# Sums of squares of queries and keys: one fp32 product with ones, or two fp32r products of a two-part split

## The chip, the cores and the metric

The kernel runs on one core of a Trainium2 chip. The metric is the device time of one execution in microseconds (us), taken as the median of several runs. Before the change it is 2640.64 us, the median of 3 runs (2636.08 to 2641.43).

Six names are used for what works side by side on the core: PE (TensorE, matrix products), PEld (TensorE's weight loads), DVE (VectorE), ACT (ScalarE), POOL (GpSimd) and SP (SyncE, which here issues the DMA transfers). Each of them works through its own list of instructions in order, and an instruction that must wait holds up all that stand behind it on the same engine.

## The reference

The reference is a two-layer backbone over 512 latent tokens and 256 context tokens. In each layer one combined input projection feeds three mixers: a neighbourhood attention, a gated DeltaNet with 4 heads of 128 channels, and a Fourier mixer; they are merged, projected, and followed by an MLP. The change lies in the DeltaNet's input, where queries and keys go through a short convolution with SiLU, are normalised to length one per head, and the latent ones are rotated:

```python
def _l2norm(x):
    xf = x.astype(jnp.float32)
    return xf * lax.rsqrt(jnp.sum(xf * xf, axis=-1, keepdims=True) + EPS)

q_l, k_l, v_l = _split(_short_conv(jnp.concatenate([dn_q, dn_k, dn_v], axis=-1), conv_w), (DN_W,) * 3)
lat_qkv = (_bhtd(_axial_rope(_l2norm(_heads(q_l, DN_HEAD_DIM)))),
           _bhtd(_axial_rope(_l2norm(_heads(k_l, DN_HEAD_DIM)))),
           _bhtd(_heads(v_l, DN_HEAD_DIM).astype(jnp.float32)))
...
k_c = _l2norm(_heads(k_c, DN_HEAD_DIM))
```

The context keys (and, in the first layer, the context queries) are normalised in the same way, without the rotation.

## The kernel before, in words

Activations lie with channels on the 128 partitions and tokens along the free dimension: 512 latent tokens and 256 context tokens, 768 in all. Large products are done in three fp32r products each (`proj`, L250 to L257): weights and inputs are split into a rounded part `hi` (ACT, L243) and a remainder `lo` (POOL or DVE, L246), both of type fp32r, and hi·hi, hi·lo and lo·hi are summed in PSUM.

A layer runs in stages. In the first stage (after L1042) the input projections of the first DeltaNet head stand beside the Fourier mixer. Then comes the mixed stage (L1059): four streams of work are written out side by side by `by_clock` (L340), which picks the stream that is least far along by the amounts that each `yield` gives: the recurrent steps of the DeltaNet (`stream_dn`), the preparation of a head with its triangular inverse (`stream_prep`, `dn_prep`), the neighbourhood attention (`stream_na`), and the input projections that feed them (`stream_in`). After it come merging, output projection and MLP, in which almost only `proj` runs. The compiler's scheduler then puts the instructions of each engine into their final order, by the priorities in which the program wrote them and by its own idea of when their inputs are ready. So a change of one instruction can move others.

`dn_in` (L523) makes one head's inputs. For the key it projects, runs `conv_silu` (L467: copy out of PSUM into `cin`, five taps on DVE, SiLU by exponentials on ACT, a last product on DVE at L482), then `l2_rope` (L485). That function squares the result on ACT (L488, into `r_l2`, 770 columns with a gap of two, or 512 where there are only latent tokens), sums the squares over the 128 channels with one fp32 product with a matrix of ones (L493: 512 columns, then 256), takes the sum to the power −1/2 by Ln and Exp on ACT (L494, L495), scales on DVE (L498, L500), and rotates (L502 to L507; the product with the sine is on POOL, L505, and that with the cosine on DVE, L506). The value goes through the convolution alone; the query goes through both again. There are 16 calls of `l2_rope`: a key and a query for each of four heads in two layers. Twelve have 770 columns; the four queries of the second layer have 512. The four calls of the two first heads lie in the first stages, twelve in the mixed ones.

The buffers with the tag `cy` (L962) hold `cin`, the result of the convolution, and `r_l2`, three in number.

Of the kernel before, what the change touches and what calls it, by code (L numbers as in the profile page):

```python
# [9 lines left out]
F32 = mybir.dt.float32  # L10
F32R = mybir.dt.float32r
AF = mybir.ActivationFunctionType
ALU = mybir.AluOpType
# [4 lines left out]
P = 128  # L18
# [28 lines left out]
def kernel(ctx: ExitStack, tc: tile.TileContext, A: dict, out: bass.AP):  # L47
    nc = tc.nc
    pe, dve, act, pool, sp = nc.tensor, nc.vector, nc.scalar, nc.gpsimd, nc.sync
# [3 lines left out]
    const = ctx.enter_context(tc.tile_pool(name="const", bufs=1))  # L53
# [12 lines left out]
    def U(name, dt=F32, tag="u", w=TT):  # L66
        b, n = cur[tag]
        return b.tile([P, w], dt, tag=tag, bufs=n, name=name)

    def T3(name):  # L70
        return U(name, tag="t3b")

    @contextmanager
    def scope(name, **bufs):
        with tc.tile_pool(name=name, bufs=1, reuse_waits="tile") as b:
            for t, n in bufs.items():
                cur[t] = (b, n)
            yield b
# [38 lines left out]
    xload(5)  # L117
    ones = const.tile([P, P], F32, name="ones")
    dve.memset(ones, 1.0)
    Tst = const.tile([P, NU, P], F32, name="Tst")  # L120
    pool.memset(Tst, 0.0)
    def sigmoid_into(dst, src):
# [252 lines left out]
    def layer(l):  # L375
# [109 lines left out]
        def l2_rope(y, w, scale, name, par):  # L485
            n = 770 if w > TL else 512
            r = U("r_l2", tag="cy", w=774)
            act.activation(out=r[:, :n], in_=y[:, :n], func=AF.Square)  # L488
            for s0, s1, o0 in ((0, TL, 0), (TL, TT, 514)):
                if s0 < w:  # L490
                    o1 = o0 + s1 - s0
                    ps = ps_aux("ps_l2")
                    pe.matmul(ps[:, 0:s1 - s0], lhsT=ones, rhs=r[:, o0:o1], start=True, stop=True)  # L493
                    act.activation(out=r[:, o0:o1], in_=ps[:, 0:s1 - s0], func=AF.Ln, bias=EPS)  # L494
                    act.activation(out=r[:, o0:o1], in_=r[:, o0:o1], func=AF.Exp, scale=-0.5)  # L495
            o = U(name, tag=name + par)
            kn = tp.tile([P, TL], F32, tag="t2", name="kn")
            dve.scalar_tensor_tensor(kn, in0=y[:, 0:TL], scalar=scale, in1=r[:, 0:TL], op0=ALU.mult, op1=ALU.mult)  # L498
            if w > TL:
                dve.scalar_tensor_tensor(o[:, TL:TT], in0=y[:, 514:770], scalar=scale, in1=r[:, 514:770],  # L500
                                         op0=ALU.mult, op1=ALU.mult)
            rot = tp.tile([P, TL], F32, tag="t2", name="rot")  # L502
            for q in range(4):
                sp.dma_start(out=rot[32 * q:32 * q + 32], in_=kn[32 * (q ^ 1):32 * (q ^ 1) + 32])
            pool.tensor_tensor(rot, rot, sinT, op=ALU.mult)  # L505
            dve.tensor_tensor(kn, kn, cosT, op=ALU.mult)  # L506
            dve.tensor_tensor(o[:, 0:TL], kn, rot, op=ALU.add)  # L507
            return o
# [450 lines left out]
                    yield 2  # L959


        mix_a = scope("mixa", **{f"{n}{i}": 1 for n in ("kT", "qT", "ktok", "vtok") for i in range(2)}, O=1, zz=1, cy=3)  # L962
        mix_a.__enter__()

        sts = [{} for _ in range(NDH)]
# [140 lines left out]
        for bi, (src, gt) in enumerate(((ofn, 16), (ona, 0), (odn, 8))):  # L1106
# [14 lines left out]
            for k in range(KD):  # L1121
# [3 lines left out]
                else:  # L1125
                    ps = inproj(T_GATE + gt + k, segs)
                    sigmoid_into(sg[:, :W], ps[:, :W])
                ada_tick(ADA_BR)
                ps = ps_main("ps_br")
                if bi == 0:  # L1130
                    proj_fn(ps, k)
                    y = ys[k] = U("y")
# [20 lines left out]
        for k in range(KD):  # L1153
# [3 lines left out]
            ps = ps_main("ps_wo")  # L1157
# [15 lines left out]
        for hb in range(4):  # L1173
            ah, al = [], []
            for k in range(8):
                ada_tick(ADA_M)
                ps = ps_main("ps_m1")
                proj(ps, wload(A["w1"][l, hb * 8 + k]), KD, mh, ml, segs)
                r = T3("rl")
# [3 lines left out]
                x, y = split_act(a[:, :W], W, "a", U)  # L1183
                ah.append(x)
                al.append(y)
            for k in range(KD):
# [3 lines left out]
                w = wload(A["w2"][l, hb, k])  # L1190
                end = hb == 3 and fin is not None

                for sg in [[s] for s in HALVES] if end and k == KD - 1 else [segs]:
                    ps = ps_main("ps_m2")
# [172 lines left out]
```

## Time and profile before

| what | value |
|---|---|
| median of 3 runs | 2640.64 us |
| profiled execution, its own time | 2641.14 us |
| span of the profiled execution | 2639.4 us |
| PE busy | 2460.9 us (93%) |
| DVE busy | 1516.9 us (57%) |
| ACT busy | 1194.3 us (45%) |
| POOL busy | 652.1 us (25%) |
| mean granted clock of TensorE | 0.974 |
| DMA, mean over the span | 106 GB/s |

The profile is of one execution. Busy time is what an engine spent in instructions, and the share is of the span. The end of a matmul is modelled, so that the duration shown for one is longer than the step from one to the next; where both are to be had, the step is what TensorE can give. "Idle before" is the time in which the engine waited just before the instructions of a group, and the name after the arrow is what ended most of that wait. The chain of waits follows the work that ended last back from the last instruction, at each step to what released it.

### The profile page before, as it was taken

What the parts mean: (1) busy time and instruction counts of PE and PEld (TensorE: products, weight loads), DVE (VectorE), ACT (ScalarE), POOL (GpSimd) and SP (SyncE); (2) the same over time, 40 slices, a digit from 0 to 9 for tenths busy, and PEclk for the clock granted to TensorE, in tenths of its full rate; (3) what the DMA queues carried; (4) which work ended last, traced back from release to release, by engine and by line L of the source; (5) the groups of instructions that cost most, each with busy time, mean ns of one, the idle gap of its engine ahead of it and who ended that gap; (6) DMA issues with size and microseconds to landing.
All of it is one profiled execution on the core that took longest, in us unless ns stands there. A gap on an engine that the chain in (4) does not pass through costs nothing.

```text
span 2639.4 us, 39034 instructions
## 1 busy us (share of the span) xinstructions
PE 2460.9 (93%) x14608; PEld 2043.2 (77%) x14608; DVE 1516.9 (57%) x2867; ACT 1194.3 (45%) x2445; POOL 652.1 (25%) x552
## 2 busy tenths in 40 slices
PE   6988989989998999999999988898889999999998
PEld 3776877777887878888888867776767777788886
DVE  5628575757457976564444473858668357433334
ACT  4545656565654233131313255555565653423333
POOL 3223222231122122111111133222242232222222
PEclk9999999999998999999999999999999999999999
DMA  7223232323155733333343313232232345233332
GB/s 223 71 80 87 69 83 61 90 79 82 63 186 166 222 121 120 118 119 120 120 128 119 117 56 97 78 86 69 82 89 74 111 134 190 78 96 96 96 96 88
DMA packets 190853, 280.89 MB, mean 106 GB/s; under 512 B 57876, under 2 KB 82200, under 8 KB 190536
## 3 DMA queue, kind: packets, MB, share of 16 engines
q1 hardware_dynamic: 190664, 278.40, 34.8%
q8 instruction: 114, 1.87, 0.3%
q14 instruction: 75, 0.61, 0.1%
HBM read 242.86 MB, written 26.03 MB: 102 GB/s over the span
## 4 chain that ended last, share of the span: by engine, by line
PE 69%; DVE 15%; ACT 5%; issue 4%; DMA 3%; POOL 2%; SPq 1%; DVEq 0%; POOLq 0%; ACTq 0%
PE ps_m L255 33%; PE ps_in L255 13%; PE ps_wo L255 4%; PE ps_inc L255 4%; PE ps_br L255 3%; DVE stmp L591 2%; DVE Wb L593 2%; DVE cy L479 2%; PE ps_s L827 1%; DVE Pm L809 1%; PE ps_ch L686 1%; PE ps_ch L682 1%; DVE xn L313 1%; PE ps_ch L704 1%; PE ps_s L821 1%
## 5 line engine op out<-in xcount | busy, mean ns | idle before, releaser
L246 POOL TENSOR_TENSOR wlo<-wr,whi 128x512 fp32r<-128x512 f32 x352 | 487.0, 1385 | 1679.8 <-ACT whi L243 1555.0
L243 ACT CAST whi<-wr 128x512 fp32r<-128x512 f32 x544 | 336.0, 619 | 778.0 <-PE ps_m L255 492.2
L255 PE MATMUL ps_in<-hh,whi 128*128 128x512 f32 x960 | 381.6, 408 | 27.1 <-ACT whi L243 21.6
L255 PE MATMUL ps_in<-hh,wlo 128*128 128x512 f32 x960 | 376.0, 402 | 2.8 <-POOL wlo L246 2.6
L255 PE MATMUL ps_in<-hl,whi 128*128 128x512 f32 x960 | 376.3, 403 | 0.0
L255 PE MATMUL ps_m<-ml,whi 128*128 128x512 f32 (+1 forms) x768 | 233.5, 358 | 4.5 <-POOL ml L323 3.9
L255 PE MATMUL ps_m<-mh,whi 128*128 128x512 f32 (+1 forms) x768 | 232.9, 358 | 4.4 <-ACT mh L319 4.4
L255 PE MATMUL ps_m<-ah,whi 128*128 128x512 f32 (+1 forms) x776 | 233.6, 354 | 0.0
L255 PE MATMUL ps_m<-ah,wlo 128*128 128x512 f32 (+1 forms) x776 | 233.2, 354 | 0.0
L255 PE MATMUL ps_m<-al,whi 128*128 128x512 f32 (+1 forms) x776 | 233.0, 354 | 0.0
L255 PE MATMUL ps_m<-mh,wlo 128*128 128x512 f32 (+1 forms) x768 | 232.1, 356 | 0.0
L255 PEld LDWEIGHTS ps_in<-hh,whi 128*128 128x128 f32 x960 | 182.2, 194 | 59.2 <-ACT whi L243 23.2
L246 DVE TENSOR_TENSOR wlo<-wr,whi 128x512 fp32r<-128x512 f32 x192 | 134.8, 702 | 139.9 <-ACT whi L243 139.9
L255 PEld LDWEIGHTS ps_in<-hh,wlo 128*128 128x128 f32 x960 | 180.4, 193 | 38.6 <-POOL wlo L246 5.4
L255 PEld LDWEIGHTS ps_in<-hl,whi 128*128 128x128 f32 x960 | 181.2, 193 | 29.9 <-issue 2.2
L1197 DVE SCALAR_TENSOR_TENSOR x<-ps_m,mod,x 128x512 f32<-128x512 f32 (+1 forms) x97 | 60.8, 654 | 215.4 <-PE ps_m L255 215.4
L202 DVE SCALAR_TENSOR_TENSOR jada<-wada,csb 128x1024 f32<-128x1024 f32 x128 | 179.6, 1403 | 0.9 <-DMA wada<-in_wat_dram 0.4
L255 PEld LDWEIGHTS ps_m<-ml,whi 128*128 128x128 f32 x768 | 127.8, 189 | 29.7 <-POOL ml L323 6.8
L255 PEld LDWEIGHTS ps_m<-mh,whi 128*128 128x128 f32 x768 | 127.7, 190 | 27.3 <-ACT mh L319 6.2
L255 PE MATMUL ps_inc<-hh,whi 128*128 128x256 f32 x512 | 148.8, 291 | 0.0
L255 PE MATMUL ps_inc<-hl,whi 128*128 128x256 f32 x512 | 148.8, 291 | 0.0
L255 PE MATMUL ps_inc<-hh,wlo 128*128 128x256 f32 x512 | 148.7, 290 | 0.0
(337 smaller groups left out, 4918.3 us busy)
## 6 DMA issues: line engine op xcount, KB each, us to landing
wr<-in_w_dram SPq DMA_DIRECT2D x256, 256.0 KB, 2.6
wr<-in_wi_dram SPq DMA_DIRECT2D x224, 256.0 KB, 2.8
wada<-in_wat_dram SPq DMA_DIRECT2D x80, 512.0 KB, 4.0
wr<-in_wb_dram SPq DMA_DIRECT2D x48, 256.0 KB, 3.0
wada<-in_wa_dram SPq DMA_DIRECT2D x32, 256.0 KB, 5.4
wr<-in_wo_dram SPq DMA_DIRECT2D x32, 256.0 KB, 2.9
gpre<-sgp SPq DMA_DIRECT2D x16, 384.0 KB, 2.3
sgg<-gpre SPq DMA_DIRECT2D x16, 384.0 KB, 4.0
```

The costliest lines, as they stand in the source:

```text
L202: pin(dve.scalar_tensor_tensor(junk, in0=ws[n], scalar=1.0, in1=cur["csb"][:, v * D:v * D + D], op0=ALU.mult, op1=ALU.mult, accum_out=MOD[ ...
L243: act.copy(hi, raw)
L246: eng.tensor_tensor(lo, raw, hi.bitcast(F32), op=ALU.subtract)
L255: pe.matmul(ps[:, s0 - off:s1 - off], lhsT=a, rhs=b[k][:, s0:s1], start=(k == 0 and i == 0), stop=(k == kn - 1 and i == 2))
L313: dve.scalar_tensor_tensor(t[:, s0:s1], in0=xs[k][:, s0:s1], scalar=sc, in1=rs[:, s0:s1], op0=ALU.mult, op1=ALU.mult)
L479: dve.scalar_tensor_tensor(y[:, :n], in0=cin[:, j:j + n], scalar=vec[:, cw + j:cw + j + 1], in1=y[:, :n], op0=ALU.mult, op1=ALU.add)
L591: dve.tensor_tensor(tv, Nb[:, j + 1:32, j:j + 1].to_broadcast([48, n, m]), Wb[:, j:j + 1, 0:m].to_broadcast([48, n, m]), op=ALU.mult)
L593: dve.tensor_tensor(Wb[:, j + 1:32, 0:m], Wb[:, j + 1:32, 0:m], tv, op=ALU.subtract)
L682: pe.matmul(ps[:, P:2 * P], lhsT=lhs, rhs=v_t, start=True, stop=True)
L686: pe.matmul(ps[:, 2 * P:3 * P], lhsT=kt, rhs=Uc, start=True, stop=True)
L704: pe.matmul(ps[:, 0:P], lhsT=st["PT"][:, d, j], rhs=Uc, start=True, stop=True)
L1197: dve.scalar_tensor_tensor(x2[k][:, s0:s1], in0=ps[:, s0:s1], scalar=mod(l, 5, k, v), in1=x2[k][:, s0:s1], op0=ALU.mult, op1=ALU.add)
```

## The change

Squares are no longer written once. ACT squares twice, into an fp32 tile (`r`) and into an fp32r tile (`rh`, which rounds). POOL subtracts the two and gives the remainder `rl`, also fp32r. The sum over channels is then two fp32r products, `rh` and `rl` with an fp32r matrix of ones, added in PSUM. One more constant is written at the start, and `cy` has four buffers instead of three in the mixed stage's scope.

```diff
@@ -117,6 +117,8 @@
     ones = const.tile([P, P], F32, name="ones")
     dve.memset(ones, 1.0)
+    ones_r = const.tile([P, P], F32R, name="ones_r")
+    act.copy(ones_r, ones)
     Tst = const.tile([P, NU, P], F32, name="Tst")
@@ -485,12 +487,18 @@
         def l2_rope(y, w, scale, name, par):
             n = 770 if w > TL else 512
             r = U("r_l2", tag="cy", w=774)
+
+            rh = U("r_hi", F32R, tag="cy", w=774)
+            rl = U("r_lo", F32R, tag="cy", w=774)
             act.activation(out=r[:, :n], in_=y[:, :n], func=AF.Square)
+            act.activation(out=rh[:, :n], in_=y[:, :n], func=AF.Square)
+            pool.tensor_tensor(rl[:, :n], r[:, :n], rh[:, :n].bitcast(F32), op=ALU.subtract)
             for s0, s1, o0 in ((0, TL, 0), (TL, TT, 514)):
                 if s0 < w:
                     o1 = o0 + s1 - s0
                     ps = ps_aux("ps_l2")
-                    pe.matmul(ps[:, 0:s1 - s0], lhsT=ones, rhs=r[:, o0:o1], start=True, stop=True)
+                    pe.matmul(ps[:, 0:s1 - s0], lhsT=ones_r, rhs=rh[:, o0:o1], start=True, stop=False)
+                    pe.matmul(ps[:, 0:s1 - s0], lhsT=ones_r, rhs=rl[:, o0:o1], start=False, stop=True)
                     act.activation(out=r[:, o0:o1], in_=ps[:, 0:s1 - s0], func=AF.Ln, bias=EPS)
@@ -959,7 +967,7 @@
-        mix_a = scope("mixa", **{f"{n}{i}": 1 for n in ("kT", "qT", "ktok", "vtok") for i in range(2)}, O=1, zz=1, cy=3)
+        mix_a = scope("mixa", **{f"{n}{i}": 1 for n in ("kT", "qT", "ktok", "vtok") for i in range(2)}, O=1, zz=1, cy=4)
```

The scheduler gives the engines another order. Three places follow; behind the names, `ps_l` is the PSUM tile of the sums, `r_l` the fp32 squares, `r_hi` and `r_lo` the two parts. Line numbers of the changed kernel are 2 higher up to `l2_rope` and 8 higher behind it.

PE, first stage of the first layer, the key of head 0, before:

```order
L255 MATMUL ps_in<-hl,whi 128x512
L493 MATMUL ps_l_583<-r_l_581,ones 128x512
L493 MATMUL ps_l_587<-r_l_581,ones 128x256
L255 MATMUL ps_in<-hh,wlo 128x512
L255 MATMUL ps_in<-hh,whi 128x512
L255 MATMUL ps_in<-hl,whi 128x512
L255 MATMUL ps_in<-hh,wlo 128x512
L255 MATMUL ps_inc<-hh,whi 128x256
```

and now:

```order
L257 MATMUL ps_in<-hh,wlo 128x512
L257 MATMUL ps_in<-hh,whi 128x512
L257 MATMUL ps_in<-hl,whi 128x512
L500 MATMUL ps_l_589<-r_hi,ones_r 128x512
L500 MATMUL ps_l_594<-r_hi,ones_r 128x256
L257 MATMUL ps_in<-hh,wlo 128x512
L257 MATMUL ps_inc<-hh,whi 128x256
L501 MATMUL ps_l_589<-r_lo,ones_r 128x512
L501 MATMUL ps_l_594<-r_lo,ones_r 128x256
```

The first products with ones stand three projection products later than the old ones, and two more projection products stand between them and the products of the remainder.

PE, mixed stage of the first layer, the query of head 1, before:

```order
L255 MATMUL ps_in<-hh,whi 128x512
L493 MATMUL ps_l_2859<-r_l_2857,ones 128x512
L255 MATMUL ps_in<-hl,whi 128x512
L255 MATMUL ps_in<-hh,wlo 128x512
L255 MATMUL ps_inc<-hh,whi 128x256
L255 MATMUL ps_inc<-hl,whi 128x256
L493 MATMUL ps_l_2863<-r_l_2857,ones 128x256
```

and now:

```order
L257 MATMUL ps_inc<-hh,wlo 128x256
L500 MATMUL ps_l_2883<-r_hi,ones_r 128x512
L257 MATMUL ps_inc<-hh,whi 128x256
L257 MATMUL ps_inc<-hl,whi 128x256
L257 MATMUL ps_inc<-hh,wlo 128x256
L257 MATMUL ps_inc<-hh,whi 128x256
L501 MATMUL ps_l_2883<-r_lo,ones_r 128x512
L257 MATMUL ps_inc<-hl,whi 128x256
```

Here the first product has moved behind two 512-column and three 256-column products of the projection, and four of 256 columns stand between the two parts.

POOL, mixed stage of the first layer, the key of head 1 and what stands behind it (`Db`, `Dl` and `Df` are the decay matrices of `dn_prep`, `rot` the rotation), before:

```order
L246 TENSOR_TENSOR wlo<-wr,whi 128x512
L550 TENSOR_TENSOR Db<-Db,n_li 128x768
L549 TENSOR_TENSOR Dl<-Df,n_li 128x768
L551 TENSOR_TENSOR Df<-Df,n_ui 128x768
L505 TENSOR_TENSOR rot<-rot,sinT 128x512
```

and now:

```order
L248 TENSOR_TENSOR wlo<-wr,whi 128x512 x2
L495 TENSOR_TENSOR r_lo<-r_l_2343,r_hi 128x770
L558 TENSOR_TENSOR Db<-Db,n_li 128x768
L473 MEMSET cin 128x2 x3
L557 TENSOR_TENSOR Dl<-Df,n_li 128x768
L559 TENSOR_TENSOR Df<-Df,n_ui 128x768
L513 TENSOR_TENSOR rot<-rot,sinT 128x512
```

The subtraction stands ahead of the decay matrices, behind the remainders of the weights.

## Rows read from the trace of the kernel before

**Rows 1.** The page, part 1: engine, busy us, share, instructions.

```profile
PE 2460.9 (93%) x14608; PEld 2043.2 (77%) x14608; DVE 1516.9 (57%) x2867; ACT 1194.3 (45%) x2445; POOL 652.1 (25%) x552
```

**Rows 2.** Busy time by stretch, core 0; the columns stand in the first row.

```profile
core 0: us, PE busy (x) PEld busy (x) DVE busy (x) ACT busy (x) POOL busy (x), PEclk, DMA share, GB/s
...
60.00:143.00 83.00, 77.91 (x484) 67.02 (x484) 47.77 (x82) 41.64 (x113) 19.28 (x34) 1.00 0.23 71
143.00:740.00 597.00, 545.80 (x3938) 457.25 (x3937) 364.67 (x879) 348.02 (x786) 152.62 (x133) 0.97 0.28 79
...
1540.00:1608.00 68.00, 61.87 (x321) 51.08 (x320) 43.21 (x67) 35.44 (x87) 18.69 (x28) 0.95 0.23 71
1608.00:2106.00 498.00, 445.60 (x3066) 355.69 (x3064) 317.65 (x767) 292.97 (x680) 149.31 (x135) 0.95 0.30 85
```

**Rows 3.** Chain of waits, first layer's first key: start us, us, what.

```profile
78.38 0.88 DVE cy L482
...
79.29 0.85 ACT r_l L488
...
80.19 1.56 PE ps_l L493 x4
```

**Rows 4.** Timeline of PE there: start us, us, engine, line, operation, names, shape.

```profile
78.42 0.39 PE L255 MATMUL ps_in<-hh,wlo 128*128 128x512 f32 x1
78.65 0.39 PE L255 MATMUL ps_in<-hh,whi 128*128 128x512 f32 x1
...
80.19 1.56 PE L493 MATMUL ps_l<-r_l,ones 128*128 128x512 f32 x4 [0.92 <-ACT r_l L488]
81.39 0.58 PE L255 MATMUL ps_in<-hh,wlo 128*128 128x512 f32 x1
...
82.86 0.28 PE L255 MATMUL ps_inc<-hh,whi 128*128 128x256 f32 x1
82.98 0.28 PE L255 MATMUL ps_inc<-hl,whi 128*128 128x256 f32 x1
```

**Rows 5.** The weight loads of L493 there, one for each pass.

```profile
80.72 0.19 PEld L493 LDWEIGHTS ps_l<-r_l,ones 128*128 128x128 f32 x1 [0.24 <-issue]
81.15 0.19 PEld L493 LDWEIGHTS ps_l<-r_l,ones 128*128 128x128 f32 x1 [0.24 <-issue]
```

**Rows 6.** The instructions of line L488 (the Square), all 16.

```profile
L488 ACT ACTIVATE r_l<-cy x16: 629/846/852, 79.3 to 1967.0; 128x770 f32<-128x770 f32 x12, 128x512 f32<-128x512 f32 x4
```

**Rows 7.** POOL's groups by shape: count, busy us, mean ns, idle before.

```profile
L323 POOL TENSOR_TENSOR ml<-xn,mh 128x768 fp32r<-128x768 f32 x4 | 8.5, 2121 | 13.6 <-ACT mh L317 13.6
...
L323 POOL TENSOR_TENSOR ml<-xn,mh 128x512 fp32r<-128x512 f32 x4 | 5.9, 1474 | 11.4 <-ACT mh L317 11.4
```

**Rows 8.** Square and first weight load of two calls in the mixed stages.

```profile
436.03 0.85 ACT L488 ACTIVATE r_l<-cy 128x770 f32<-128x770 f32 x1 [0.53 <-DVE cy L482]
436.93 0.30 PEld L493 LDWEIGHTS ps_l<-r_l,ones 128*128 128x128 f32 x2
...
1806.98 0.85 ACT L488 ACTIVATE r_l<-cy 128x770 f32<-128x770 f32 x1
...
1809.20 0.55 PEld L493 LDWEIGHTS ps_l<-r_l,ones 128*128 128x128 f32 x2
```

**Rows 9.** Chain of waits, first layer, at head 1's key and at its query.

```profile
246.93 1.27 POOL wlo L246
248.19 6.03 issue
...
309.20 1.13 PE ps_l L493 x2
```

**Rows 10.** Timeline of DVE and of POOL during one rotation.

```profile
87.47 2.11 POOL L505 TENSOR_TENSOR rot<-rot,sinT 128x512 f32<-128x512 f32 x1 [3.46 <-DMA rot<-kn]
...
88.35 1.78 DVE L506 TENSOR_TENSOR kn<-kn,cosT 128x512 f32<-128x512 f32 x1
```

**Rows 11.** All 16 instructions of L506 on DVE: shortest, median, longest in ns.

```profile
L506 DVE TENSOR_TENSOR kn<-kn,cosT x16: 673/689/1780, 88.4 to 1978.5; 128x512 f32<-128x512 f32 x16
```

## The prediction, on record before the run

> **What bounds the kernel now.** I begin with the busy shares [rows 1]: PE is busy for 93% of the span, no other engine for more than 57%. So time that PE loses is lost to the kernel unless PE would have waited there anyway, and work on ACT or POOL costs nothing by itself. Then the stretches [rows 2]. The change acts in four of them: the two first stages (60 to 143 us and 1540 to 1608 us) and the two mixed stages (143 to 740 us and 1608 to 2106 us). In the mixed ones PE is busy for 545.8 of 597 and 445.6 of 498 us; the 104 us left are what could hide a wait of PE, and all that another cover can be found in. Last the chain of waits around one call [rows 3]: DVE finishes the convolution, ACT squares for 0.85 us, PE runs the product with ones, and the chain stays on PE. PE had stood idle for 0.92 us until the square came [rows 4]. That is the place to look at: a call has PE waiting for a chain of DVE and ACT, and the change makes that chain longer while it makes PE's own part shorter.
>
> **The change part by part.**
>
> *The product.* The old product makes two passes over its columns; the weight loads of the 512 columns and the 256 columns follow each other by 0.43 us [rows 5]. From its start at 80.19 us to the next projection product at 81.39 us PE gives 1.20 us to 512 and 256 columns [rows 4]; 512 alone take 2 × 0.43 = 0.86 us. An fp32r product steps by 0.23 us for 512 columns and by 0.12 us for 256 [rows 4], so two of each take 2 × (0.23 + 0.12) = 0.70 us, and two of 512 take 0.46 us. The saving is 0.50 us in twelve calls and 0.40 us in four, 12 × 0.50 + 4 × 0.40 = **7.6 us** of PE's time.
>
> *The second Square.* It stands on ACT right behind the first. The shape decides: 0.85 us in twelve calls, 0.63 us in four [rows 6], 12.7 us in all. ACT is busy for under 60% of the mixed stages [rows 2], so as work it costs nothing; as a step in the chain it counts in full, for both products now need its result or what POOL makes of it.
>
> *The subtraction on POOL.* The trace has the same operation: fp32 minus fp32r into fp32r takes 2.12 us for 768 columns and 1.47 us for 512 [rows 7]. That makes 12 × 2.12 + 4 × 1.47 = 31.3 us on an engine that is busy for under a third of the mixed stages [rows 2]; as work it costs nothing.
>
> *The chain of a call.* Before: the square ends, 0.05 us of handing on, then 1.20 us of PE. After: 0.85 us for the second Square, 0.05, 2.12 for the subtraction, 0.05, then the second pair of products, 0.35 us. The products of `rh` run beside POOL. PE is free of the call 0.85 + 0.05 + 2.12 + 0.05 + 0.35 = 3.42 us after the first Square instead of 1.25 us, **2.17 us later**; with 512 columns it is 0.63 + 0.05 + 1.47 + 0.05 + 0.23 = 2.43 against 0.91 us, 1.52 us later. The saved 7.6 us are inside these numbers.
>
> *What PE does meanwhile.* The order has moved some products ahead of those of the remainder. For the first key four of 512 columns and one of 256 come first, 4 × 0.23 + 0.12 = 1.04 us, and 2.17 − 1.04 = 1.13 us stay; the first query of that layer has the same order. In the second layer the first key has three products of 256 columns between, and 1.81 us stay; its query has one of 512 and seven small ones (taken at 0.12 us, as 256 columns), about 0.9 us, and 0.6 us stay. The four calls in the first stages give 1.13 + 1.13 + 1.81 + 0.6 = **4.7 us**.
>
> The other twelve calls are in the mixed stages: nine of 770 columns and three of 512, 9 × 2.17 + 3 × 1.52 = 24.1 us. The products that the order puts ahead add up over the twelve to 8.9 us by the same steps (between none for the key of head 1 in the first layer and 1.3 us for its query). From this comes off how late PE arrived: the first weight load of L493 begins 0.05 to 1.37 us after the Square's end, 4.5 us over the twelve (the two ends stand in [rows 8]); in that much PE had other work. 24.1 − 8.9 − 4.5 = **10.7 us**. Not all of it lengthens the stage. At the key of head 1 in the first layer the chain goes by POOL and a long wait instead [rows 9], and wherever PE waits soon after for DVE or ACT, the delay is absorbed. Between none and all of it I take half, 5.3 us, since the chain stands on PE's products in eight of the twelve places, as at the query of head 1 [rows 9], and PE idles for 9% of these stages.
>
> *The fourth buffer and the constant.* A call now takes three tiles of `cy` instead of one. With four of them the value's `cin` still finds a free one while the key's call runs, so I cost it at nothing. Without that buffer the value's projection would stay in PSUM until the call ends. One copy of 128 columns at the start, beside DMA, costs nothing.
>
> *The queues moved past.* The subtraction stands in POOL's queue ahead of decay matrices and of weight remainders. It must wait for ACT there, up to 0.9 us plus its own 2.1 us, and what stands behind it is late by as much. POOL mostly waits for ACT's `whi` anyway; PE's products with `wlo` come last of three. No cost by itself. Nor is the rest of the new order: the mixed stages are shuffled throughout, and one wait like the 6.03 us [rows 9] more or less would move the sum by as much; I leave that to the range.
>
> **Sum.** 4.7 + 5.3 = +10.0 us on the profiled execution's 2641.14 us, which stands 0.5 us above the median: **2651 us**. With PE's delays all on the path it is 4.7 + 10.7 = 15.4 us, 2656 us; with none of them it is the rival that comes next.
>
> **The rivals.**
>
> *Faster: the saving shows, the chain doesn't.* If ACT and POOL get far enough ahead of PE, the remainder is there when PE comes to it, and what is left is the 7.6 us of PE's time, 2641 − 8 = 2633 us. This decides where PE arrives more than 3 us after the first Square. For it speaks that PE is the bound and that the new order has shifted products; against it that in the twelve calls PE was late by 0.05 to 1.37 us alone [rows 8], and idle at the first key [rows 4].
>
> *No change.* The mixed stages may be held by the heads' chain through DVE, POOL and DMA [rows 9], with the delays swallowed and the 4.7 us of the first stages set against savings later: 2641 us, within some 5 us. For it speaks PE's idle 104 us.
>
> *Slower still: POOL holds DVE up.* While POOL worked on `rot` from 87.47 to 89.58 us, the product with the cosine on DVE, which reads two tiles in SBUF, took 1.78 us [rows 10], against a median of 0.69 us [rows 11]; it ended 0.55 us after POOL did. So a POOL subtraction may cost DVE up to 1.1 us each. If that falls on DVE work in the chain (taps, inverse) in all 16 calls, it adds 16 × 1.1 = 17 us: 2668 us. Against it: DVE's next step in the same stream needs the call's result and has not started. The Trainium skill, SBUF — State Buffer, section "Who interferes with whom", says that a DVE instruction with two inputs in SBUF contends with a GpSimd instruction that reads SBUF, and that the loser blocks for the whole instruction. By that rule this rival is the rule's outcome, 2668 us; the pair in rows 10 agrees with it.
>
> *The change does not do what it says.* If an fp32r product with ones ran at the fp32 step, nothing would be saved, and 0.50 us come on top for each call, some 8 us. The 0.23 us step is of fp32r products of the same shape, so I give this no chance of its own.
>
> **How the numbers follow.** About 0.2%, 5.3 us, is what a measurement of this kernel can tell from no change. Forecast (PE waits in part of the calls): 0.44. POOL holding DVE up on top: 0.10. No change: 0.28. Saving alone: 0.18. So slower 0.54, same 0.28, faster 0.18. The forecast's own range, from its first stages alone to all of PE's delay, is 2646 to 2657 us. The range for 8 in 10 takes in the saving at 2633 us, and at the top the lock in its full size with a little for the shuffled order: 2632 to 2670 us.
>
> **What would show it.** The products with ones should follow each other by 0.23 and 0.12 us, and their group's busy time should fall. PE should wait for `r_lo`, by 1 to 2 us in most of the 16 calls, and the chain should go from the Square to POOL's subtraction to PE. The first stages should be longer by 4 to 5 us in sum. If PE waits for `r_lo` in few calls, the forecast is wrong and the first rival right; if DVE's two-input instructions beside `r_lo` take over 1.5 us and stand on the chain, the third. If MLP or merge stages differ, I have missed something altogether.

## The result: 1.3% slower, and outside the range

The changed kernel takes **2674.61 us** (median of 3 runs, 2673.31 to 2679.34) against 2640.64 us: ratio 1.013, 95% interval 1.011 to 1.015, that is +34 us (29 to 40). The forecast was 2651 us, the top of the range 2670 us. The direction was right, the size was three times too small. The profiled execution took 2679.34 us, its span is 2677.6 us, the mean granted clock 0.968 (before 0.974).

The page, part 1, of the changed kernel (as [rows 1]):

```profile
PE 2476.4 (92%) x14608; PEld 2055.2 (77%) x14608; DVE 1530.0 (57%) x2867; ACT 1206.6 (45%) x2462; POOL 676.6 (25%) x568
```

PE is busy for 15.5 us *more*, though its work became less, and idle for 22.7 us more. Busy time by stretch, with the columns of [rows 2] and the bounds moved to the same events:

```profile
60.00:148.50 88.50, 80.37 (x486) 69.86 (x484) 47.38 (x82) 42.90 (x113) 21.82 (x36) 0.96 0.22 66
148.50:772.00 623.50, 562.84 (x3940) 469.57 (x3939) 366.26 (x879) 352.45 (x793) 157.42 (x139) 0.94 0.27 75
1566.50:1636.70 70.20, 62.85 (x331) 51.27 (x332) 47.85 (x72) 39.24 (x93) 23.29 (x32) 0.98 0.23 71
1636.70:2145.00 508.30, 448.87 (x3066) 357.62 (x3064) 327.42 (x767) 297.33 (x686) 164.19 (x138) 0.95 0.30 83
```

The four stretches grew by 5.5, 26.5, 2.2 and 10.3 us. The clock of the first fell from 1.00 to 0.96 and of the second from 0.97 to 0.94, and there PE's busy time grew most; in the third it rose (0.95 to 0.98), in the fourth it stayed. The new instructions (engine, operation, names, count, shortest/median/longest in ns, first and last start, shapes), and who waited for the subtraction:

```profile
L494 ACT ACTIVATE r_hi<-cy x16: 612/830/841, 80.6 to 2000.7; 128x770 fp32r<-128x770 f32 x12, 128x512 fp32r<-128x512 f32 x4
...
L495 POOL TENSOR_TENSOR r_lo<-r_l,r_hi x16: 1262/1825/1914, 81.6 to 2001.4; 128x770 fp32r<-128x770 f32 x12, 128x512 fp32r<-128x512 f32 x4
...
  PE ps_l L501: 13.4, 11
```

The second Square lasts about as long as the first (0.83 us against 0.85); the subtraction takes 1.83 us instead of the 2.12 us that I took. At the first key PE looks like this (as [rows 4]; in brackets the idle time before and what ended it):

```profile
80.14 0.39 PE L257 MATMUL ps_in<-hl,whi 128*128 128x512 f32 x1
81.50 0.61 PE L500 MATMUL ps_l<-r_hi,ones_r 128*128 128x512 f32 x2 [0.97 <-ACT r_hi L494]
81.95 0.40 PE L257 MATMUL ps_in<-hh,wlo 128*128 128x512 f32 x1
82.19 0.28 PE L257 MATMUL ps_inc<-hh,whi 128*128 128x256 f32 x1
83.48 0.62 PE L501 MATMUL ps_l<-r_lo,ones_r 128*128 128x512 f32 x2 [1.01 <-POOL r_lo L495]
83.94 0.28 PE L257 MATMUL ps_inc<-hl,whi 128*128 128x256 f32 x1
...
84.17 0.41 PE L257 MATMUL ps_inc<-hh,whi 128*128 128x256 f32 x1
84.38 0.42 PE L257 MATMUL ps_inc<-hl,whi 128*128 128x256 f32 x1
84.59 0.41 PE L257 MATMUL ps_inc<-hh,wlo 128*128 128x256 f32 x1
```

PE waits for the second Square, runs what stands between, and waits again for the subtraction, as forecast. But then the products of 256 columns step by 0.21 us; before, and again from 87.6 us on, the step is 0.12 us. The granted clock, the third value from the end in these rows of 2 us, says why:

```profile
80.00:82.00 2.00, 1.02 (x6) 0.56 (x5) 0.00 (x0) 1.45 (x2) 0.42 (x1) 1.00 0.26 99
82.00:84.00 2.00, 0.99 (x6) 0.62 (x6) 0.00 (x0) 0.54 (x1) 1.60 (x4) 1.00 0.00 0
84.00:86.00 2.00, 2.00 (x12) 2.00 (x12) 0.56 (x1) 1.71 (x5) 0.00 (x0) 0.54 0.00 0
86.00:88.00 2.00, 2.00 (x13) 2.00 (x12) 1.16 (x3) 0.62 (x1) 0.16 (x3) 0.60 0.13 33
```

Behind two waits of about 1 us each, PE ran for over 3 us mostly at the lower of its two levels (1.2 instead of 2.4 GHz), and lost 2.00 × 0.46 + 2.00 × 0.40 = 1.7 us. The kernel before has one wait here, and keeps 1.00:

```profile
80.00:82.00 2.00, 1.81 (x6) 1.24 (x7) 0.00 (x0) 0.78 (x3) 0.00 (x0) 1.00 0.06 20
82.00:84.00 2.00, 2.00 (x16) 1.86 (x16) 1.02 (x2) 1.52 (x4) 0.14 (x3) 1.00 0.00 0
84.00:86.00 2.00, 2.00 (x16) 1.91 (x16) 0.69 (x1) 1.12 (x2) 0.01 (x1) 1.00 0.26 66
```

The chain that ended last, in the second layer, passes through the subtraction at two calls; one of them:

```profile
1964.68 0.74 ACT r_hi L494
1965.49 1.92 POOL r_lo L495
1967.46 0.52 PE ps_l L501
```

**An account of PE's time.** From rows like these, 4 us each, I add up for the two first and two mixed stages PE's idle time (4 us less busy) and the time lost to the clock (busy × (1 − granted clock)); what is left of a stage's growth is work. A stage runs from its first Square, or from POOL's first `Dl` (mixed), to the next stage or, for a mixed one, to the merge. All against before (1206.1 us, of which 111.7 idle and 28.8 lost to the clock), in us; the last columns are from 2 us rows, idle / lost in the 12 us around each of the 16 calls alone:

| kernel | four stages | idle | clock | work | at the calls: idle / clock |
|---|---|---|---|---|---|
| before | 0 | 0 | 0 | 0 | 13.6 / 3.6 |
| changed | +43.6 | +20.7 | +24.7 | −1.8 | 32.8 / 20.2 |
| `hi_only` | −1.6 | +0.5 | +10.5 | −12.6 | 15.6 / 13.0 |
| `change_old_order` | +28.8 | +14.3 | +18.4 | −3.9 | 29.3 / 23.6 |
| `before_new_order` | +14.9 | +7.5 | +6.7 | +0.7 | 18.7 / 6.4 |

The account is coarse: each row is the difference of two single executions. What `hi_only` (below) leaves out of PE's work is 12 × 0.85 + 4 × 0.63 = 12.7 us by [rows 4, 5], and the column gives 12.6 us. But `sq2`, `side_tiny` and `tiny_act` (below) change nothing in PE's work, and the same column, taken from their profiles, gives +5.8, +5.7 and +4.5 us. So it is good to some 6 us, and −1.8 us can't be told from nothing. The stages outside took 5.4 us less in the changed kernel's profiled execution than in before's; between the 16 profiles (without the four kernels near 3,560 us, below) they differ by up to 7 us.

The clock can also be read without stages, since each execution has its span and its mean granted clock on record. Span × (1 − granted clock), idle time included, has these means over a kernel's executions. The last column is the kernel before, run beside it; for the changed kernel it is the lowest and the highest of these means:

| kernel | executions | granted clock | span × (1 − clock), us | before, us |
|---|---|---|---|---|
| changed | 3 | 0.968 | 85.6 | 70 to 73 |
| `hi_only` | 10 | 0.972 | 73.5 | 70.4 |
| `warm` | 4 | 0.973 | 71.4 | 70.4 |
| `change_old_order` | 4 | 0.968 | 86.7 | 70.1 |
| `before_new_order` | 6 | 0.974 | 70.3 | 70.1 |

Over the whole kernel the clock thus costs the change some 14 us of the 34, not 24.7: before's profiled execution lost some 10 us more to the clock outside the four stages than the changed kernel's did. And of the +10.5 and +6.7 us that the account has for `hi_only` and `before_new_order`, 3 us and nothing are left. A single profile's clock column, at the calls too, can thus be off by several us.

### The profile page after: what moved, and what is told of

Read it like the earlier page. It is cut to its first block, busy times and chain, and to the rows that moved or that the text cites. A ratio compares the mean times of both kernels' runs of the same rounds, so it can differ in the third digit from the quotient of the medians.

```text
span 2677.6 us, 39084 instructions
## 1 busy us (share of the span) xinstructions
PE 2476.4 (92%) x14608; PEld 2055.2 (77%) x14608; DVE 1530.0 (57%) x2867; ACT 1206.6 (45%) x2462; POOL 676.6 (25%) x568
## 5 line engine op out<-in xcount | busy, mean ns | idle before, releaser
L257 PEld LDWEIGHTS ps_in<-hh,whi 128*128 128x128 f32 x960 | 184.0, 196 | 56.1 <-ACT whi L245 18.4
```

The lines of the kernel that those rows point to most:

```text
L257: pe.matmul(ps[:, s0 - off:s1 - off], lhsT=a, rhs=b[k][:, s0:s1], start=(k == 0 and i == 0), stop=(k == kn - 1 and i == 2))
```

## Experiments

The open question is whether the 34 us are PE's waits, the clock behind them, POOL beside DVE, or the order of the mixed stages.

**The product of the rounded part alone, and the subtraction on DVE**

```diff
-            act.activation(out=r[:, :n], in_=y[:, :n], func=AF.Square)
...
-            pool.tensor_tensor(rl[:, :n], r[:, :n], rh[:, :n].bitcast(F32), op=ALU.subtract)
...
-                    pe.matmul(ps[:, 0:s1 - s0], lhsT=ones_r, rhs=rl[:, o0:o1], start=False, stop=True)
```

> The changed kernel with one fp32r product of the rounded squares alone: the fp32 Square, the subtraction on POOL and the products of the remainder are left out, so the sums lack the remainder. Theory clock (PE's waits for the remainder, and the lower granted clock of TensorE that follows each of them, make the loss): no wait for r_lo is left, the granted clock comes back to 0.974 or more, and the time falls to 2628 to 2642 us, the kernel before less some 8 us. Rival order (the new order of the mixed stages makes the loss): still a shuffled order, 2655 to 2680 us. Rival lock (POOL's subtraction holds DVE up): also back to 2628 to 2642 us.

`hi_only`: 2633.84 us against 2641.11, ratio 0.9975 (0.9962 to 0.9987): faster than both kernels, for sums of rounded squares. The time is the one that theory clock and rival lock share. The granted clock came back to 0.972, not to the 0.974 expected; the order is a new one here too. Of the 12.7 us of PE's work that it leaves out (4 × 0.63 and 12 × 0.85), 7 us arrive.

```diff
-            pool.tensor_tensor(rl[:, :n], r[:, :n], rh[:, :n].bitcast(F32), op=ALU.subtract)
+            dve.tensor_tensor(rl[:, :n], r[:, :n], rh[:, :n].bitcast(F32), op=ALU.subtract)
```

> The changed kernel with the subtraction on DVE instead of POOL, where it should take 0.95 to 1.05 us for 770 columns instead of 1.85. Theory clock: the second wait of PE shrinks by some 0.9 us in most calls, the stretches of low clock get fewer, 2648 to 2665 us. Rival order: within 5 us of 2675 us, or anything if the order changes again. Rival lock: nothing of POOL is left to hold DVE up, 2640 to 2655 us.

`dve_sub`: 2653.99 us, 1.0055 (1.0034 to 1.0075), in the ranges of theory clock and of the lock. PE waits for the remainder for 1.5 us in 3 places instead of 13.4 us in 11, and over half of the loss is gone. In its first stages no time is lost to the clock (3.1 + 1.6 us in the changed kernel). The order differs from the changed kernel's, so the shorter wait is not shown to be the whole reason.

**A longer chain alone, and PE kept at work during the wait**

```diff
             act.activation(out=r[:, :n], in_=y[:, :n], func=AF.Square)
+            act.activation(out=r[:, :n], in_=y[:, :n], func=AF.Square)
```

> The kernel before with its Square run twice on ACT, one behind the other, and all else as before: the chain to the fp32 product is 0.85 us longer (0.63 us in four calls) without fp32r, POOL, or more buffers. Theory clock: PE waits longer before its product, one wait of up to 1.8 us; where that brings the clock down the call costs 1.5 us more than the wait; 2646 to 2662 us, granted clock 0.970 to 0.974. If waits alone cost, at most 12.7 us: 2641 to 2653 us. Rival order and rival lock: 2641 us but for what the scheduler shuffles.

`sq2`: 2649.42 us, 1.0031 (1.0015 to 1.0047), which both ranges hold; the product stays the old one. With four Squares:

> The kernel before with its Square run four times: the chain to the fp32 product is 2.55 us longer (1.9 us in four calls), somewhat more than the changed kernel's 2.17 us, in one wait of PE. Theory clock: the first stages lose clock behind each of their calls, PE idles 15 to 25 us more and loses as much again by clock: 2662 to 2685 us. If only the wait itself costs: 2648 to 2662 us. Rival order, rival lock: near the 2649 us of the run with two Squares.

`sq4`: 2663.75 us against 2644.01, 1.0077 (1.0059 to 1.0096), 20 us more without POOL and without new products. The time is as theory clock had it, its way is not: the first layer's first stage loses nothing to the clock, and PE waits at the product for 5.4 us in 7 places, where before it waits for 8.4 us in 6. So the 20 us are not waits at the product, and what the longer chain costs and what the new order costs are not separated here. Then the changed kernel with six more products while PE waits, whose sums are overwritten:

```diff
+                    for _ in range(6 if s0 == 0 else 0):
+                        pe.matmul(ps[:, 0:s1 - s0], lhsT=ones_r, rhs=rh[:, o0:o1], start=True, stop=True)
```

> The changed kernel with six more products of the rounded squares with ones in front of the real one, each overwritten by the next (512 columns, 1.4 us in all), which stand where PE waits for the remainder. They do no useful work. Theory clock: PE no longer idles there, the clock stays at its upper level behind most calls, the granted clock rises from 0.968 to 0.974 or more, and the time falls by 10 to 22 us although PE has 22 us more to do: 2652 to 2665 us. Rival order, rival lock: no fall, 2675 to 2695 us.

`warm`: 2671.72 us, 1.0111 (1.0085 to 1.0138). In sum it is a miss for both theories: it is 3 us under the changed kernel, and the intervals overlap. But 96 more products of 0.23 us, 22 us of PE's time, cost nothing, and at the first key the clock stays up:

```profile
82.00:84.00 2.00, 1.90 (x10) 1.28 (x9) 0.00 (x0) 0.29 (x1) 1.21 (x4) 1.00 0.00 0
84.00:86.00 2.00, 2.00 (x18) 2.00 (x17) 0.87 (x2) 2.00 (x6) 0.09 (x3) 1.00 0.00 0
```

Around the calls the loss to the clock falls from 20.2 to 8.8 us, and the granted clock is back at 0.973 in the mean of four executions, that of before. At the first key this pair shows that the second wait brings the lower clock. For the whole kernel it agrees with that, though the order differs here too. The account gives `warm` against before about +7 us of idle time, +10 of clock and +20 of work: what is won in idle time and clock is spent on the added products.

**POOL's and ACT's work, with nobody waiting for it.** The kernel before, with the second Square and a subtraction that nothing reads (its tiles, the constant and the fourth buffer are left out here):

```diff
             act.activation(out=r[:, :n], in_=y[:, :n], func=AF.Square)
+            act.activation(out=rh[:, :n], in_=y[:, :n], func=AF.Square)
+            pool.tensor_tensor(rl[:, :n], y[:, :n], rh[:, :n].bitcast(F32), op=ALU.subtract)
```

> The second Square on ACT and the subtraction on POOL (of the convolution's result and the rounded squares, so its value means nothing) are issued as in the changed kernel, with four buffers, but nobody reads them; the sums come from the fp32 product of the fp32 squares as before. Theory clock: the work by itself costs nothing, PE waits as before: 2636 to 2648 us. Rival lock: 16 POOL instructions of 1.85 us hold DVE up, 2650 to 2660 us. Rival order: the mixed stages are in a new order here too, so anything between 2640 and 2675 us; a time near 2641 us speaks against it.

`side_work`: 2665.72 us, 1.0082 (1.0066 to 1.0099), inside the order's range and above the lock's. This looked like POOL after all; the next three say that it isn't. The same on two columns:

> As the run with unread work (second Square and subtraction, four buffers, fp32 product), but both work on two columns alone, so that the same instructions take next to no time. Theory work: back to 2636 to 2646 us. Theory order: 2646 to 2670 us, within what other orders give.

`side_tiny`: 2651.76 us against 2642.45, 1.0047 (1.0027 to 1.0067): over 9 us for next to no work, with another order. Its order is not `side_work`'s either, so the 14 us between the two are not shown to be order: the second Square as a load on ACT is left as a rival for them. Then four buffers alone, and with them POOL's subtraction alone (`y` − `y`, unread), two kernels whose engines work in the same order in the traces:

> The kernel before with four cy buffers in place of three and nothing else. The scheduler gives the mixed stages another order. Theory order (the mixed stages of the kernel before stand in an order that suits the chip, and any change of it costs time by idle PE and lower clock): 2646 to 2665 us although no work is added. Theory work (what ACT, POOL or the chain have more to do costs the time): 2636 to 2644 us.

> The run before it (four buffers, fp32 product) with one POOL subtraction of 770 or 512 columns in each call that nobody reads, and no second Square. The order of all other instructions is nearly that of the run before it, so the two tell POOL's work apart from the order. Rival lock: 5 to 17 us over the run before it, DVE's instructions with two SBUF inputs longer. Theory order: within 4 us of the run before it.

`before_cy4`: 2639.41 us, 0.999 (0.9978 to 1.0002), and `side_pool`: 2640.47 us, 0.9996 (0.9984 to 1.0009). The mixed stages of both stand in another order than before's, and this one costs nothing; so not every new order does, as theory order had it. Part 1 of `side_pool`'s page:

```profile
PE 2463.8 (93%) x14608; PEld 2043.4 (77%) x14608; DVE 1518.0 (58%) x2867; ACT 1195.2 (45%) x2446; POOL 672.2 (25%) x568
```

POOL works 20.1 us more than in [rows 1], and it costs nothing. POOL as a load, and the lock, fall; of ACT's second Square this pair says nothing. With the subtraction made in the chain of Ln, but not of PE (it reads `r`, over which Ln then writes):

> As the run before it, but POOL subtracts the rounded squares from the fp32 squares, which Ln then overwrites: so Ln, Exp and what follows on DVE wait for POOL as in the changed kernel, while PE's fp32 product waits for the first Square alone. Theory clock: without a longer wait of PE there is no loss of clock, 2638 to 2652 us. If the late kT and qT make the loss (chain of the heads), 2655 to 2675 us.

`pe_free`: 2661.68 us, 1.0069 (1.0052 to 1.0087). This is in the range of the rival: late `kT` and `qT`, which the heads' chain needs, make the loss. It is also 4 us under `side_work`, where nothing waits for POOL, in yet another order. So it separates the late results neither from the order nor from the waits, and the heads' chain stays a rival for a part of the loss.

**The order.** One copy of two columns on ACT in each call, read by nobody:

```diff
+            junk = tp.tile([P, 2], F32, tag="jk", name="jk")
+            act.copy(junk, y[:, 0:2])
```

> The kernel before with one more copy of two columns on ACT in each call, read by nobody, three buffers: some 1.5 us of ACT in all, another order in the mixed stages. Theory order: 2645 to 2665 us. Theory work: 2638 to 2645 us.

`tiny_act`: 2657.91 us, 1.0065 (1.0046 to 1.0084). 16 tiny copies move the time by 15 us, and the one other difference is that the scheduler orders the mixed stages anew. And the changed kernel with the products of the remainder given a lower priority, so that more stands between:

```diff
+                    tc.cur_priority += 200
                     pe.matmul(ps[:, 0:s1 - s0], lhsT=ones_r, rhs=rl[:, o0:o1], start=False, stop=True)
+                    tc.cur_priority -= 200
```

> The changed kernel with a lower priority for the products of the remainder alone: in the two first stages some 25 to 40 projection products now stand between the two parts, in the mixed stages the order hardly gives them more room. Theory clock: the first stages fall by 3 to 6 us (first layer, from the first call's Square to the first decay matrix, from 76.5 to about 71 us) with no clock lost there; in the mixed stages within 6 us of the changed kernel; 2660 to 2675 us. Rival order and rival lock: the first stages stay as they are, since POOL's work is the same.

`after_late200`: 2687.61 us, 1.0168 (1.0153 to 1.0184), above the one range given: a miss. PE's idle time in the first layer's first stage falls from 7.2 to 4.8 us, but the stage only from 76.5 to 75.3 us, and the second layer's first stage goes from 55.6 to 64.8 us, with 16.2 us of PE idle instead of 6.1.

**Order and waits taken apart.** An order can be held by tying each instruction of an engine to the one ahead of it, without a wait between them:

```diff
+    for chain in orders:
+        for a, b in zip(chain, chain[1:]):
+            tc.add_manual_dep(at[b], a, mybir.DependencyInfo(mybir.DependencyClass.NoSync, mybir.DependencyReason.DATA),
+                              reason="order")
```

In the first four such kernels the list was the wrong one: the order in which the program is written, not that of the built kernel.

> The changed kernel, with PE's instructions held in the order that they have in the kernel before; the 28 products of the remainder are free, and the scheduler puts each directly behind the product of the rounded part with the same columns, so that no projection product stands between the two as cover. DVE, ACT, POOL and SP then have the order of before too, apart from the new instructions. Theory A (the new order of the mixed stages costs most of the 34 us): what is left is PE waiting for the second Square and for the subtraction, without cover: by the lengths of the chain 12 x 2.17 + 4 x 1.52 = 32 us less the 4.5 us by which PE came late anyway, if all of it lies on the path, half of that if the mixed stages absorb half; 2652 to 2665 us. Theory B (the waits and the lower clock behind each of them cost the 34 us, and the order costs nothing): the waits are longer here than in the changed kernel, because nothing covers them, so 2680 us or more.

> The kernel before, with PE's instructions held in the order that they have in the changed kernel; the fp32 product stands where the changed kernel has the product of the rounded part. The other engines then have the changed kernel's order as well. No work is added and nothing new is waited for. Theory A (order): PE waits and runs at the lower clock in the mixed stages as it does in the changed kernel, so 2655 us or more, with the excess between the two layers' first stages and their ends and not in the first stages. Theory B (waits for the remainder): 2641 us, within 5 us.

> The product of the rounded part alone (one fp32r product; the fp32 Square, the subtraction and the products of the remainder are left out, so the sums are of rounded squares), in PE's order of before. With its own order this kernel took 2633.8 us. PE's work is less by 12 x 0.85 + 4 x 0.63 = 12.7 us at most (the old product less one fp32r product), and nothing waits longer. Theory A: the order is that of before, so it gains what PE can use of the 12.7 us and nothing is lost to a new order: 2630 to 2637 us. Theory B: the same as with its own order, 2634 us. It tells how much of PE's saved time reaches the end when nothing is reordered.

> As the changed kernel in the order of before, with the subtraction on DVE instead of POOL; with its own order that kernel took 2654.0 us. The wait is shorter by POOL's duration less DVE's, about 1 us a call, and the other orders are those of before. Theory A: nearer to before than its own order, 2645 to 2652 us, and 8 to 15 us under the changed kernel in the order of before if PE's waits count in full. Theory B: 2655 to 2665 us, since the products of the remainder have no cover here.

3575.63, 3562.61, 3535.22 and 3565.02 us, all near 1.35 times before. Neither theory is tried by them, and they stand here for one number: the scheduler's order is worth over 900 us, so that a shuffle of it can well cost 1%. With the right lists:

> All five engines held in the order in which the built kernel before has them (the four runs ahead of this one were held in the order in which the program is written, not in that of the built kernel before); the second Square, the subtraction and the products of the remainder are put in between by the scheduler, which leaves up to four products between the two parts, as in the changed kernel. So that this order can be kept with four buffers of cy, the remainder is written over the first Square's tile, and that tile is of type fp32r: the first Square and the reciprocal root are rounded to fp32r, and the remainder is zero. Counts and shapes of the instructions are those of the changed kernel. Theory A (the new order costs most of the 34 us): what is left is PE's waits, 2645 to 2658 us. Theory B (the waits and the lower clock behind them cost it, and the order nothing): 2668 to 2680 us. If both count half, 2658 to 2668 us.

> The kernel before, with four buffers of cy, all five engines held in the order in which the built changed kernel has them; the fp32 product stands where the changed kernel has the product of the rounded part. No work is added. Theory A (order): 2655 to 2672 us, the excess in the mixed stages, as waits of PE and as lower clock, and the first stages not longer by more than 2 us. Theory B (waits for the remainder): 2636 to 2646 us. If the order is at its worst only together with the waits, both this run and the one beside it are under 2658 us.

**2669.27 us, 1.0103 (1.0088 to 1.0118)** for `change_old_order` and **2655.76 us, 1.0051 (1.0036 to 1.0067)** for `before_new_order`, before 2641.53. In the traces the engines follow the orders that they were given. The change's instructions alone, in the old order, cost 27 us (23 to 31); the new order alone costs 13 us (10 to 18). Together the changed kernel shows 34 us (29 to 40), so the two overlap in part, or just add up within the intervals. The first number lies where theory B had it, the second where theory A had it: each cause is there by itself, neither theory holds alone, and the change's own instructions are the larger share. Held in before's order they lower the granted clock from 0.974 to 0.968, which is 17 of their 27 us (86.7 less 70.1); held in the new order the kernel before keeps 0.974. All that the account has for `change_old_order` lies around the calls, +15.7 us of idle time and +20.0 us of clock. In `change_old_order` the lower clock is again seen behind the waits, where [rows 3]'s call runs in the same order as before:

```profile
80.00:82.00 2.00, 1.08 (x4) 0.60 (x4) 0.00 (x0) 0.63 (x1) 1.29 (x1) 1.00 0.01 2
82.00:84.00 2.00, 1.41 (x4) 1.17 (x5) 0.00 (x0) 0.80 (x3) 0.54 (x1) 0.72 0.00 0
84.00:86.00 2.00, 2.00 (x11) 1.97 (x10) 1.03 (x2) 1.36 (x4) 0.17 (x3) 0.50 0.00 0
```

This is not so behind every call: at the first layer's first query of the same kernel PE waits for 1.78 and 0.81 us, and the granted clock stays at 1.00. And the lower clock can last. At the query of the second layer's second head PE waits for `r_hi` and `r_lo` (0.22 and 0.39 us by the timeline) after a wait of 0.52 us, and is at half clock for at least the next 10 us, of which these are the first 6; what keeps it there is not shown:

```profile
1750.00:1752.00 2.00, 1.39 (x11) 0.78 (x5) 0.86 (x1) 1.93 (x5) 1.28 (x1) 1.00 0.65 80
1752.00:1754.00 2.00, 1.79 (x13) 1.18 (x12) 0.42 (x1) 1.94 (x5) 0.00 (x0) 0.50 1.00 146
1754.00:1756.00 2.00, 2.00 (x8) 1.59 (x7) 0.69 (x1) 0.93 (x3) 0.00 (x0) 0.50 0.76 219
1756.00:1758.00 2.00, 2.00 (x14) 1.35 (x13) 0.00 (x0) 0.00 (x0) 0.73 (x1) 0.50 0.49 175
```

Three limits of this pair: the old order can't be kept with three tiles of `cy` in a call, so `change_old_order` writes the remainder over the first Square, which rounds that Square and leaves a remainder of zero; the order of the new instructions among the old ones is still the scheduler's; and the waits are not the changed kernel's, for `r_hi` 16.2 us in 13 places and for the remainder 11.7 us in 14, against 5.1 us in 7 and 13.4 us in 11.

## Why the prediction was wrong, step by step

*PE as the bound, and the place to look at.* Right for the place: around the calls lie most of PE's added idle time and of the clock lost in the four stages. POOL's added work costs nothing (`side_pool`); that ACT's does not is argued, not shown.

*The saving on the product, 7.6 us.* Too large. The steps are 0.23 and 0.12 us in a row, but behind a wait the pair of 512 and 256 columns takes 0.45 us (81.50 to 81.95, and 83.48 to 83.94), not 0.35: two pairs 0.91 us against 1.20, so 0.29 us saved at the first key, not 0.50. What is saved over all 16 calls is not shown: the account's −1.8 and −3.9 us are within its error.

*The chain of a call.* Right within 0.3 us: the subtraction is shorter (1.83 instead of 2.12 us), the pairs of products longer.

*What PE does meanwhile.* Right at the first key, and near in the sum by luck. At the first key the waits are 0.97 + 1.01 us against 0.92 us before, 1.06 us more where I had 1.13. The forecast's net 4.7 + 5.3 us, with the 7.6 us of saved work that it contains, means 17.6 us more idle time; the profile has 20.7 us in the four stages, 19.2 us of it around the calls. But by stages it is not right: with the saving taken out I had 6.6 us in the first stages and 11.0 in the mixed ones, and the profile has 4.0 and 16.5. The new order by itself adds 10 us of idle time in the mixed stages and takes 4 us off in the first ones (`before_new_order`), which the forecast left out. The half that I took for the mixed stages was a guess, and no run shows it. Of the terms that it stands on, the twelve delays of PE taken off as 4.5 us add up to 4.3 us in the trace.

*The failed step: a wait was priced at its length and nothing else.* "PE is free of the call ... 2.17 us later", and the sum stops there. Time lost to the clock has no term, though the clock of 0.97 and 0.95 in the mixed stages stood in [rows 2] and showed that PE already runs at the lower level for a part of them. It measured some 14 us over the whole kernel in all executions (85.6 against 70 to 73 us), and +24.7 us in the four stages of the two profiled ones, +16.6 us of it around the calls. So in the profiled pair the clock cost about as much as the added idle time (20.7 us, 19.2 us of it around the calls); over all executions it cost less. From the forecast's +10.0, 3.1 us more of idle time, 5.8 us less saved (within the account's error) and 24.7 us of clock make the 43.6 us of the account.

*The second failed step: the new order.* "No cost by itself. Nor is the rest of the new order ... I leave that to the range." By itself it costs 13 us (`before_new_order`), in the account as idle time (+7.5 us) and lower clock (+6.7 us); over all executions its clock is that of before, so the lower clock is not borne out. `tiny_act` shows that as much comes of a change that does next to nothing. The range left it one wait of 6 us. Of three new orders for nearly the same work, one (`before_cy4`, and `side_pool` with it) lies within 0.1% of before and two (`side_tiny`, `tiny_act`) 0.5 and 0.65% above; that width belonged in the range, upward above all.

*The rivals.* "The saving shows" fell, because PE waits for the remainder, 13.4 us in 11 places; its number, 2633 us, is what `hi_only` takes, where the chain is no longer than before; but that kernel leaves out 12.7 us of PE's work, not 7.6. "No change" fell with the intervals. "POOL holds DVE up" fell by `side_pool`: sixteen subtractions beside DVE, ratio 0.9996 (0.9984 to 1.0009). The Trainium skill, SBUF — State Buffer, section "Who interferes with whom", would have it that the loser of the shared ports stands still for a whole instruction; single instructions may do so, as [rows 10] show, but in the time of `side_pool` nothing of it shows.

What stays open: why the order of before is good, that is which of the shuffled pieces brings the 13 us; how far the two causes add up rather than overlap; and, within the 27 us of the instructions, what part comes from late keys and queries (`pe_free`) or from ACT's second Square rather than from PE's waits and the clock behind them.

## What to carry to other kernels

Where TensorE is the bound, price a new wait of it twice: once for its length, and once for the slower stretch that may follow, which here cost some 14 us of the 34. Less work for PE is no gain when it is bought with a longer chain ahead of PE: the same kernel gained 0.25% where the rounded product came without the remainder, and lost 1.3% with it. And where a scheduler orders a stage anew, run a change that does nothing (a copy of two columns) beside the real one, or hold the order; without that, a per cent can't be put down to the change's instructions.

## What the runs showed of the hardware that I had not expected

Two waits of PE of 0.97 and 1.01 us, 1 us of products between them, were followed by granted clocks of 0.54 and 0.60 for 4 us; one wait of 0.92 us at the same place was followed by 1.00, and so was the first of the two when six more products filled the second (`warm`). But two waits of 1.78 and 0.81 us at the first query of `change_old_order` were followed by 1.00 as well; no run shows what decides. POOL's subtraction of 770 columns took 1.83 us by the profile, quicker than the 2.12 us of the 768 columns in [rows 7]. And 16 copies of two columns on ACT came with 15 us more, where the order is the one other difference.
